# Gate/up product of a decoder block with its weights as the stationary operand and the tokens streamed

## The chip, the cores and the metric

The kernel runs on one core of a Trainium2 chip. The metric is the device time of one execution in microseconds (us), the median of three runs. Engines are named as the profile names them: PE is the matrix engine (PEld its weight loads), DVE, ACT and POOL work element by element, SP issues the loads of the weights.

A matmul on PE has two operands. The **stationary** one, a 128 x 128 tile, is loaded into the array first; the **moving** one is streamed through it, column by column. The result appears in PSUM, with one row for each column of the stationary tile and one column for each column of the moving operand.

## The reference

One decoder block for 256 tokens of width 1024: a convolution branch and an attention branch, merged and added to the input, and then the feed-forward part that the change is about.

```
h = h + merged @ w_out
n = h * rsqrt(mean(h * h) + EPS) * norm2_g
h = h + (silu(n @ w_gate) * (n @ w_up)) @ w_down      # w_gate, w_up: 1024 x 2816; w_down: 2816 x 1024
```

## The kernel before

**Three products for one.** All weights are float32. Each operand is split into a high part (rounded to the matmul type float32r) and a low part (the rest), and a product is summed from three matmuls: high by high, low by high, high by low. `mm3` issues them (L141, L142, L143).

**Slots.** The weights arrive in 146 pieces of 512 KB, 128 partitions by 1024 values, one for each slot. A list of slots, written out once, sets the order of all work. In each slot PE does 12 matmuls: two k-tiles, two token tiles, three matmuls each. Here a 128 x 128 tile of the tokens is stationary and 512 columns of a weight piece are streamed. Slots 0 to 79 are the products of the two branches and the out projection (80 x 12 = 960 such matmuls), slots 80 to 123 the gate/up product (528), and slots 124 to 145 the down product (246, and 36 with 256 columns, tile `end`, which finish the last block).

**Splitting.** ACT writes a piece's high part (`whi`, L123), DVE or POOL the low part (`wlo`, L124), six slots ahead of PE, into eight buffers each. In the built program these buffers lie 4,096 bytes apart in a partition.

**Between the products.** The out projection's result is added to the residual `xs`, transposed on PE (`htr`, L513) and split into `hh` and `hl` (L518, L519). The second norm's factor for each token, `rstd2`, comes from sums of squares on ACT (L525), one addition on DVE (L527) and two instructions on POOL (L178, L179). It is applied after the gate/up product, where a token is a row of the result, so the factor is one number for each partition.

**After a gate/up chunk.** Each chunk has 256 gate and 256 up columns. ACT takes silu of the gate half (L546), DVE multiplies (L548), giving `f` with tokens on the partitions. The down product wants `f` with its features on the partitions, so PE transposes it (`ftr`, L560, four in each of 11 chunks), and ACT and DVE split the result into `fh` and `fl` (L561, L562). The first two chunks are done in halves, so that h^T's second half may come later.

**Other work that the texts name.** `store` adds the down product to `xs` and writes the output (L571, L572). `ident` is the identity tile for transposes.

Of the kernel before, what the change touches and what calls it, by code (L numbers as in the profile page):

```python
# [26 lines left out]
G = 2  # L27
EPS = 1e-6
BIG = 1e30
# [11 lines left out]
SPL_BUFS = 8  # L41
AHEAD = 6
# [13 lines left out]
class Chunk:  # L56
    """CW output columns of one product, for all tokens: nk k-tiles in pieces of G."""

    def __init__(self, name, w, lhs, nk, done):
        self.name, self.w, self.lhs, self.nk, self.done = name, w, lhs, nk, done  # L60
        self.acc = None


@with_exitstack
def hybrid_block(ctx: ExitStack, tc: tile.TileContext, x, xT, par, w_in, w_co, w_ao, w_o, w_gu, w_dn, out):
# [20 lines left out]
    def add(*chunks):  # L86
        """One chunk, or two of which each half is done in turn."""
        n = chunks[0].nk // G
# [7 lines left out]

    def parts(i):
        return [slice(j, j + 1) for j in range(G)] if i < 3 else [slice(0, G)]

    def stream_dma(upto):  # L100
        while at["dma"] < min(upto, len(slots)):
            i = at["dma"]
            c, g = slots[i]
            raw[i] = wp.tile([P, G, CW], F32, tag="raw", bufs=RAW_BUFS, name=f"raw{i}")
# [8 lines left out]
    def stream_split(upto):  # L113
        while at["split"] < min(upto, len(slots)):
            i = at["split"]
            hi[i] = wp.tile([P, G, CW], F32R, tag="whi", bufs=SPL_BUFS, name=f"whi{i}")
            lo[i] = wp.tile([P, G, CW], F32R, tag="wlo", bufs=SPL_BUFS, name=f"wlo{i}")
            r = raw.pop(i)
            eng = nc.gpsimd if on_pool(i) else nc.vector
            for part in parts(i):  # L120
                if i == 0:
                    split_x(part.start)
                nc.scalar.copy(hi[i][:, part, :], r[:, part, :])  # L123
                eng.tensor_sub(lo[i][:, part, :], r[:, part, :], hi[i][:, part, :].bitcast(F32))  # L124
            at["split"] += 1
# [7 lines left out]
    def mm3(c, i, g, t, acc=None, cols=slice(0, CW), first=0, last=None):  # L133
        """Piece g of the chunk for token tile t; the sum runs from k-tile first to last."""
        xh, xl = c.lhs()
        acc = c.acc[t] if acc is None else acc
        last = c.nk - 1 if last is None else last
        tok = slice(t * P, (t + 1) * P)
        for j in range(G):
            k = g * G + j  # L140
            nc.tensor.matmul(acc, xh[:, k, tok], hi[i][:, j, cols], start=(k == first), stop=False)  # L141
            nc.tensor.matmul(acc, xl[:, k, tok], hi[i][:, j, cols], start=False, stop=False)  # L142
            nc.tensor.matmul(acc, xh[:, k, tok], lo[i][:, j, cols], start=False, stop=(k == last))  # L143

# [6 lines left out]
    warm = cst.tile([P, CW], BF16, name="warm")  # L151
# [7 lines left out]
    wps = bank("wps", CW)  # L159
    for _ in range(WARM):  # L160
        nc.tensor.matmul(wps, warm[:, :P], warm, start=True, stop=True)
# [14 lines left out]
    def rsqrt_mean(o, ss, n, width):  # L176
        """o = (ss / n + EPS) ** -0.5"""
# [27 lines left out]
    def refill(ch):  # L205
        """The channels of the next tile go on the partitions, after KC - 1 zeros."""
# [288 lines left out]
    s2 = sm.tile([P, T, 2], F32, bufs=1, name="s2")  # L495

    def out_done(b):
        cols = slice(b * CW, (b + 1) * CW)

        def done(slot, acc):  # L500
# [21 lines left out]
            def squares():  # L522
# [13 lines left out]
    ff = {}  # L536

    def ffn_done(c):
        def done(slot, acc):
            f = {}  # L540

            def gate():
                for t in range(T):
                    r = rstd2[:, t : t + 1]
                    sg = sm.tile([P, 256], F32, tag="e0", name=f"fs{c}{t}")
                    nc.scalar.activation(sg, acc[t][:, :256], AF.Silu, scale=r)  # L546
                    f[t] = sm.tile([P, 256], F32, tag="e1", name=f"f{c}{t}")
                    nc.vector.scalar_tensor_tensor(f[t], acc[t][:, 256:], r, sg, op0=ALU.mult, op1=ALU.mult)  # L548

            def turn():  # L550
                if not ff:
                    early.close()
                    late_pool = ctx.enter_context(tc.tile_pool(name="ff", bufs=1))
                    ff[0] = (late_pool.tile([P, KF, S], F32R, name="fh"), late_pool.tile([P, KF, S], F32R, name="fl"))
                fh, fl = ff[0]
                k2 = slice(2 * c, 2 * c + 2)
                tr = bank(f"ftr{c}", 2, S)
                for j in range(2):
                    for t in range(T):
# [4 lines left out]
            pre[slot + 1].append(gate)  # L564
            jobs[slot + 2].append(turn)
        return done
# [27 lines left out]
    ffn = [Chunk(f"gu{c}", w_gu[c], lambda: hT[0], KD, ffn_done(c)) for c in range(FF // 256)]  # L594
    add(*ffn[:2])
    for c in ffn[2:]:
        add(c)
# [26 lines left out]
    def square(q):  # L624
        """Squares of x, summed over the parts of its rows that share a partition."""
# [37 lines left out]
    for slot, (c, g) in enumerate(slots):  # L663
        for job in pre.pop(slot, ()):
            job()
        if g == 0:
            c.acc = [ps.tile([P, CW], F32, tag="mm", bufs=4, name=f"{c.name}_{t}") for t in range(T)]
        if slot < n - tail:
            mm3(c, slot, g, 0)
# [4 lines left out]
        if slot < n - tail:  # L674
            mm3(c, slot, g, 1, last=split_k - 1 if c is slots[-1][0] else None)
            if slot == n - tail - 1:
                nc.vector.tensor_add(xs[:, 1, D - CW :], xs[:, 1, D - CW :], c.acc[1])
# [17 lines left out]
        if g == c.nk // G - 1:  # L695
# [50 lines left out]
```

## Time and profile before

| | |
|---|---|
| median of 3 runs | 446.02 us (445.62 to 446.3) |
| span of the profiled execution | 443.5 us |
| time before and after that span, against the median | 2.5 us |
| PE busy | 437.6 us (99%), 2026 matmuls and as many loads |
| DVE, ACT, POOL busy | 309.6, 243.9, 87.5 us |

The profiled execution's own time is its span of 443.5 us from the first to the last instruction; the 2.5 us lie around it. A matmul's duration in the profile includes its way through the array, so what a stream of them costs is read from the distance between two starts. The chain of work that ended last says what the end of the program hangs on.

### The profile page before, as it was taken

The page shows a single profiled execution, that of the slowest core. Times are in us where ns is not written, and L with a number is a line of the kernel's source. Part 1 is how long each engine was busy: PE and PEld are TensorE (multiplying, and loading weights), DVE is VectorE, ACT ScalarE, POOL GpSimd, SP SyncE. Part 2 cuts the span into 40 slices and gives each one's busy share as a digit, 9 for nine tenths or more (in the row PEclk, how much of TensorE's full clock was granted, in tenths as well). Part 3 has the DMA queues.
Part 4 walks back from the last instruction along what each step waited for, and adds up shares of the span by engine and source line. Part 5 has one row for each costly group of instructions (what it writes and reads, how often), then busy time and mean ns, then how long its engine had stood idle before and what let it go on. Part 6 is the DMA issues. An engine that isn't in the chain of part 4 may idle for free.

```text
span 443.5 us, 5743 instructions
## 1 busy us (share of the span) xinstructions
PE 437.6 (99%) x2026; PEld 359.6 (81%) x2026; DVE 309.6 (70%) x523; ACT 243.9 (55%) x439; POOL 87.5 (20%) x73
## 2 busy tenths in 40 slices
PE   8999999999999999999999999999999999999997
PEld 4788888888888888888888888888888888888886
DVE  5989999898899799967586575555555555644501
ACT  6854466689998676639325374444444444633200
POOL 1614465745462443100000000000000000000000
PEclk9999999999999999999999999999999999999999
DMA  8986684355345444544837337655555555585001
GB/s 274 345 271 213 211 303 150 144 185 197 142 149 185 142 137 150 190 163 161 293 95 247 133 120 253 196 189 184 184 185 179 187 181 184 184 252 204 25 0 49
DMA packets 23340, 80.21 MB, mean 181 GB/s; under 512 B 2576, under 2 KB 3216, under 8 KB 23312
## 3 DMA queue, kind: packets, MB, share of 16 engines
q1 hardware_dynamic: 22896, 78.66, 52.9%
q10 hardware_dynamic: 416, 1.19, 0.8%
q8 instruction: 16, 0.26, 0.3%
q14 instruction: 12, 0.10, 0.1%
HBM read 78.79 MB, written 1.05 MB: 180 GB/s over the span
## 4 chain that ended last, share of the span: by engine, by line
PE 94%; POOL 2%; ACT 2%; DMA 1%; SPq 0%; issue 0%; DVE 0%
PE gu L141 9%; PE gu L143 9%; PE gu L142 9%; PE dn L141 4%; PE dn L143 4%; PE dn L142 4%; PE g L143 3%; PE g L142 3%; PE g L141 3%; PE conv L141 2%; PE conv L143 2%; PE conv L142 2%; PE k L143 2%; PE v L143 2%; PE q L143 2%; PE q L141 2%
## 5 line engine op out<-in xcount | busy, mean ns | idle before, releaser
L124 DVE TENSOR_TENSOR wlo<-raw,whi 128x1024 fp32r<-128x1024 f32 (+1 forms) x125 | 153.0, 1256 | 30.5 <-ACT whi L123 29.6
L123 ACT CAST whi<-raw 128x1024 fp32r<-128x1024 f32 (+1 forms) x149 | 148.9, 1035 | 34.9 <-PE dn L142 19.8
L221 DVE SCALAR_TENSOR_TENSOR cacc<-cv,prm,cacc 128x256 f32<-128x256 f32 x240 | 97.2, 475 | 0.2
L141 PE MATMUL gu<-whi,hh 128*128 128x512 f32 x176 | 69.6, 395 | 0.0
L124 POOL TENSOR_TENSOR wlo<-raw,whi 128x1024 fp32r<-128x1024 f32 x24 | 58.1, 2426 | 54.5 <-ACT whi L123 49.6
L143 PE MATMUL gu<-wlo,hh 128*128 128x512 f32 x176 | 68.7, 390 | 0.0
L142 PE MATMUL gu<-whi,hl 128*128 128x512 f32 x176 | 68.5, 389 | 0.0
L143 PEld LDWEIGHTS gu<-wlo,hh 128*128 128x128 f32 x176 | 33.0, 188 | 7.1
L142 PEld LDWEIGHTS gu<-whi,hl 128*128 128x128 f32 x176 | 33.1, 188 | 6.6
L141 PEld LDWEIGHTS gu<-whi,hh 128*128 128x128 f32 x176 | 33.1, 188 | 6.4
L141 PE MATMUL dn<-whi,fh 128*128 128x512 f32 x82 | 32.5, 396 | 0.0
L143 PE MATMUL dn<-wlo,fh 128*128 128x512 f32 x82 | 32.4, 396 | 0.0
L142 PE MATMUL dn<-whi,fl 128*128 128x512 f32 x82 | 32.4, 396 | 0.0
L546 ACT ACTIVATE fs<-gu,rstd 128x256 f32<-128x256 f32 x22 | 10.4, 475 | 39.1 <-PE gu L143 39.1
L548 DVE SCALAR_TENSOR_TENSOR f<-gu,rstd,fs 128x256 f32<-128x256 f32 x22 | 10.6, 484 | 29.1 <-ACT fs L546 29.1
L141 PE MATMUL conv<-whi,xgh 128*128 128x512 f32 x64 | 26.1, 409 | 0.9 <-ACT whi L123 0.8
L141 PE MATMUL g<-whi,xgh 128*128 128x512 f32 x64 | 26.6, 415 | 0.0
L142 PE MATMUL conv<-whi,xgl 128*128 128x512 f32 x64 | 25.4, 398 | 0.0
L143 PE MATMUL conv<-wlo,xgh 128*128 128x512 f32 x64 | 25.4, 397 | 0.0
L143 PE MATMUL g<-wlo,xgh 128*128 128x512 f32 x64 | 25.2, 394 | 0.0
L142 PE MATMUL g<-whi,xgl 128*128 128x512 f32 x64 | 25.0, 391 | 0.0
L561 ACT CAST fh<-ftr 128x512 fp32r<-128x512 f32 x11 | 6.5, 587 | 23.9 <-PE ftr L560 23.9
(159 smaller groups left out, 746.4 us busy)
## 6 DMA issues: line engine op xcount, KB each, us to landing
raw<-in_w_in SPq DMA_DIRECT2D x53, 512.0 KB, 4.2
raw<-in_w_gu SPq DMA_DIRECT2D x44, 512.0 KB, 4.3
raw<-in_w_dn SPq DMA_DIRECT2D x22, 512.0 KB, 4.1
raw<-in_w_ao SPq DMA_DIRECT2D x8, 512.0 KB, 3.3
raw<-in_w_co SPq DMA_DIRECT2D x8, 512.0 KB, 3.3
raw<-in_w_o SPq DMA_DIRECT2D x8, 512.0 KB, 5.1
raw<-in_w_in SPq DMA_DIRECT2D x6, 256.0 KB, 4.7
xs<-in_x ACTq DMA_DIRECT2D x1, 1024.0 KB, 4.7
```

Source lines behind the costliest of these rows:

```text
L123: nc.scalar.copy(hi[i][:, part, :], r[:, part, :])
L124: eng.tensor_sub(lo[i][:, part, :], r[:, part, :], hi[i][:, part, :].bitcast(F32))
L141: nc.tensor.matmul(acc, xh[:, k, tok], hi[i][:, j, cols], start=(k == first), stop=False)
L142: nc.tensor.matmul(acc, xl[:, k, tok], hi[i][:, j, cols], start=False, stop=False)
L143: nc.tensor.matmul(acc, xh[:, k, tok], lo[i][:, j, cols], start=False, stop=(k == last))
L221: nc.vector.scalar_tensor_tensor(cacc[j], src, w, cacc[j], op0=ALU.mult, op1=ALU.add)
L546: nc.scalar.activation(sg, acc[t][:, :256], AF.Silu, scale=r)
L548: nc.vector.scalar_tensor_tensor(f[t], acc[t][:, 256:], r, sg, op0=ALU.mult, op1=ALU.mult)
L561: nc.scalar.copy(fh[:, k2, :], tr)
```

## The change

The gate/up product is turned around. The 128 x 128 tiles of the weights become the stationary operand and h^T (`hh`, `hl`, 256 tokens) is streamed. A result tile then has 128 features on the partitions and 256 tokens along the row: the layout that the down product wants. There are 44 such column tiles, alternately gate and up, each the sum over 8 k-tiles and 3 matmuls: 1056 matmuls of 256 columns. A piece holds eight weight tiles, so a slot has 24 matmuls.

- The transposes `ftr` go. What follows a column tile is: gate times factor (`scaled`), silu, product with the up tile, high part, low part.
- The factor of the second norm is now one number for each column. `spread2` on POOL makes an all-ones tile and two diagonal tiles of `rstd2`, one matmul (`rb`, plain float32) turns them into a row for all partitions, and ACT copies it. It is applied to the gate alone; the up part's factor is applied at the end, in `store`.
- The first six column tiles take their first four k-tiles in slots 80 to 82 and the rest in slots 83 to 85; six PSUM banks are used in turn, two of them those of the convolution.
- The 16 buffers of split weights are 4,160 bytes apart, so that their addresses go through 0, 64, 128, ... modulo 512. In the built program `hh` moves from 0 to 256 modulo 512, and `fh` from 32 bytes past a multiple of 64 to a multiple of 64.
- A few small tiles change size (`warm`, `s2`).

```diff
+GU_BANKS = ("cv0", "cv1", "mm", "mm", "mm", "mm")
+GU_ORDER = halves_first(2 * KF, KD, len(GU_BANKS))
...
+    def spl(part, i):
+
+        u, n = shape_of(i)
+        t = wp.tile([P, G * CW + STEP], F32R, tag=f"w{part}{i % SPL_BUFS}", name=f"w{part}{i}")
+        return t[:, : G * CW].rearrange("p (u n) -> p u n", n=n)
...
-            hi[i] = wp.tile([P, G, CW], F32R, tag="whi", bufs=SPL_BUFS, name=f"whi{i}")
-            lo[i] = wp.tile([P, G, CW], F32R, tag="wlo", bufs=SPL_BUFS, name=f"wlo{i}")
+            hi[i], lo[i] = spl("hi", i), spl("lo", i)
...
+    def mm_cols(c, i, g, units, slot):
+        xh, xl = c.rhs()
+        for u in units:
+            n, k = c.order[g * U + u]
...
+            nc.tensor.matmul(acc, hi[i][:, u, :], xh[:, k, :], start=first, stop=False)
+            nc.tensor.matmul(acc, hi[i][:, u, :], xl[:, k, :], start=False, stop=False)
+            nc.tensor.matmul(acc, lo[i][:, u, :], xh[:, k, :], start=False, stop=last)
...
+                    spread2()
+                    jobs[slot + 4].append(row2)
...
-                    nc.scalar.activation(sg, acc[t][:, :256], AF.Silu, scale=r)
-                    nc.vector.scalar_tensor_tensor(f[t], acc[t][:, 256:], r, sg, op0=ALU.mult, op1=ALU.mult)
...
-                        nc.tensor.transpose(tr[:, j, t * P : (t + 1) * P], f[t][:, j * P : (j + 1) * P], ident)
-                nc.scalar.copy(fh[:, k2, :], tr)
-                nc.vector.tensor_sub(fl[:, k2, :], tr, fh[:, k2, :].bitcast(F32))
...
+    def spread2():
+
+        allone, diag = sm.tile([P, P], F32, tag="junk", name="allone"), free("diag")
+        nc.gpsimd.memset(allone, 1.0)
+        for t in range(T):
+            nc.gpsimd.tensor_scalar_mul(diag[:, t * P : (t + 1) * P], ident, rstd2[:, t : t + 1])
...
+    def row2():
+        rb = bank("rb", S)
+        nc.tensor.matmul(rb, second["ones"], second["diag"], start=True, stop=True)
+        second["row"] = free("row2", "kT")
+        nc.scalar.copy(second["row"], rb)
...
+            nc.vector.tensor_mul(st["g"], acc, second["row"])
...
+            nc.scalar.activation(st["s"], st["g"], AF.Silu)
...
+            nc.vector.tensor_mul(st["f"], acc, st["s"])
...
+            nc.scalar.copy(ff[0][0][:, j, :], st["f"])
...
+            nc.vector.tensor_sub(ff[0][1][:, j, :], st["f"], ff[0][0][:, j, :].bitcast(F32))
...
-        nc.vector.tensor_add(o, acc, xs[:, t, to])
+        nc.vector.scalar_tensor_tensor(o, acc, rstd2[:, t : t + 1], xs[:, t, to], op0=ALU.mult, op1=ALU.add)
```

On PE, inside the gate/up product, before (slot 83; `f` is the product of gate and up with tokens on the partitions):

```order
L141 MATMUL gu_0_2648<-whi_2658,hh 128x512
L142 MATMUL gu_0_2648<-whi_2658,hl 128x512
L143 MATMUL gu_0_2648<-wlo_2659,hh 128x512
L560 MATMUL ftr_2766<-ident,f_2724 128x128
L560 MATMUL ftr_2766<-ident,f_2728 128x128
L560 MATMUL ftr_2766<-ident,f_2724 128x128
L560 MATMUL ftr_2766<-ident,f_2728 128x128
L141 MATMUL gu_1_2649<-whi_2658,hh 128x512
```

and of the changed kernel, in the middle of slot 83, where the one extra matmul `rb` stands:

```order
L191 MATMUL gu_2585<-hh,whi_2531 128x256
L192 MATMUL gu_2585<-hl,whi_2531 128x256
L193 MATMUL gu_2585<-hh,wlo_2532 128x256
L606 MATMUL rb<-diag,allone 128x256
L191 MATMUL gu_2604<-hh,whi_2531 128x256
L192 MATMUL gu_2604<-hl,whi_2531 128x256
L193 MATMUL gu_2604<-hh,wlo_2532 128x256
```

The moving operand stands first behind the arrow: it was the weights, and is h^T now. The four transposes are gone, and `rb` stands 84 matmuls behind the product's first.

On POOL, the last work of the program, before and then now (`lr` belongs to the convolution's norm):

```order
L178 TENSOR_SCALAR lr<-mv 128x2
L179 TENSOR_TENSOR lr<-lr,mhalf 128x2
L178 TENSOR_SCALAR rstd_112<-rstd_112 128x2
L179 TENSOR_TENSOR rstd_112<-rstd_112,mhalf 128x2
L742 UNCONDITIONAL_BRANCH
```

```order
L231 TENSOR_TENSOR lr<-lr,mhalf 128x2
L230 TENSOR_SCALAR rstd_112<-rstd_112 128x2
L231 TENSOR_TENSOR rstd_112<-rstd_112,mhalf 128x2
L599 MEMSET allone 128x128
L601 TENSOR_SCALAR diag<-ident,rstd_112 128x128 x2
L831 UNCONDITIONAL_BRANCH
```

Three instructions now follow the factor on POOL, and `rb` on PE reads what they write.

On DVE, in the middle of the gate/up product, before and then now (`wlo` is the split of a later piece):

```order
L548 SCALAR_TENSOR_TENSOR f_2959<-gu_0_2876,rstd_112,fs_2957 128x256
L548 SCALAR_TENSOR_TENSOR f_2963<-gu_1_2877,rstd_112,fs_2961 128x256
L124 TENSOR_TENSOR wlo_2976<-raw_2856,whi_2975 128x1024
L124 TENSOR_TENSOR wlo_2994<-raw_2884,whi_2993 128x1024
L562 TENSOR_TENSOR fl<-ftr_2997,fh 128x512
L124 TENSOR_TENSOR wlo_3019<-raw_2902,whi_3018 128x1024
L124 TENSOR_TENSOR wlo_3037<-raw_2927,whi_3036 128x1024
```

```order
L617 TENSOR_TENSOR fg_2936<-gu_2903,row_2731 128x256
L157 TENSOR_TENSOR wlo_2954<-raw_2759,whi_2953 128x1024
L625 TENSOR_TENSOR f_2971<-gu_2938,fs_2969 128x256
L157 TENSOR_TENSOR wlo_2989<-raw_2795,whi_2988 128x1024
L635 TENSOR_TENSOR fl<-f_2971,fh 128x256
L617 TENSOR_TENSOR fg_3006<-gu_2973,row_2731 128x256
L157 TENSOR_TENSOR wlo_3024<-raw_2840,whi_3023 128x1024
L625 TENSOR_TENSOR f_3041<-gu_3008,fs_3039 128x256
```

Before, four splits came with three other instructions; now two come with three, and the three stand apart.

## Rows read from the trace of the kernel before

**Rows 1.** The page: busy time, granted clock by slice, chain that ended last.

```profile
PE 437.6 (99%) x2026; PEld 359.6 (81%) x2026; DVE 309.6 (70%) x523; ACT 243.9 (55%) x439; POOL 87.5 (20%) x73
...
PEclk9999999999999999999999999999999999999999
...
PE 94%; POOL 2%; ACT 2%; DMA 1%; SPq 0%; issue 0%; DVE 0%
```

**Rows 2.** Stretches: length, then PE, PEld, DVE, ACT, POOL busy, granted clock.

```profile
5.60:252.50 246.90, 246.25 (x1156) 203.90 (x1157) 210.35 (x412) 160.63 (x328) 84.75 (x58) 1.00 0.57 197
252.50:378.00 125.50, 125.50 (x579) 103.91 (x578) 73.30 (x85) 62.38 (x89) 0.89 (x2) 1.00 0.58 183
378.00:435.80 57.80, 57.80 (x251) 46.57 (x250) 23.62 (x22) 18.43 (x19) 0.00 (x0) 1.00 0.38 124
435.80:440.20 4.40, 4.40 (x37) 4.20 (x35) 1.12 (x2) 0.00 (x0) 0.00 (x0) 1.00 0.24 89
```

**Rows 3.** Timeline of PE in the gate/up product (start us, us).

```profile
299.81 0.39 PE L141 MATMUL gu<-whi,hh 128*128 128x512 f32 x1
...
302.30 0.39 PE L143 MATMUL gu<-wlo,hh 128*128 128x512 f32 x1
302.53 0.60 PE L560 MATMUL ftr<-ident,f 128*128 128x128 f32 x4
```

**Rows 4.** Timeline of PE in the down product.

```profile
400.80 0.40 PE L141 MATMUL dn<-whi,fh 128*128 128x512 f32 x1
...
402.20 0.40 PE L141 MATMUL dn<-whi,fh 128*128 128x512 f32 x1
```

**Rows 5.** Timeline of PE in the last 36 matmuls.

```profile
435.80 0.28 PE L141 MATMUL end<-whi,fh 128*128 128x256 f32 x1
...
439.94 0.28 PE L143 MATMUL end<-wlo,fh 128*128 128x256 f32 x1
```

**Rows 6.** The chain, pieces of the f transposes (start us, us, what).

```profile
291.32 0.44 PE ftr L560 x4
...
370.85 0.44 PE ftr L560 x4
```

**Rows 7.** Timeline of PE, transposes of the out projection.

```profile
256.65 1.04 PE L513 MATMUL htr<-ident,xs 128*128 128x128 f32 x8
257.44 0.48 PE L141 MATMUL gu<-whi,hh 128*128 128x512 f32 x1
```

**Rows 8.** Groups by line: weight loads of the eight warm-up matmuls.

```profile
L161 PEld LDWEIGHTS <-warm 128*128 128x128 bf16 x8 | 1.0, 141 | 2.8 <-issue 1.7 <-DVE warm L152 1.2
```

**Rows 9.** The chain, a plain float32 matmul of the scores.

```profile
91.50 0.43 PE sc L388 x2
```

**Rows 10.** Timeline of POOL, the second norm.

```profile
262.26 0.19 POOL L178 TENSOR_SCALAR rstd<-rstd 128x2 f32<-128x2 f32 x1 [67.14 <-DVE rstd L527]
262.54 0.69 POOL L179 TENSOR_TENSOR rstd<-rstd,mhalf 128x2 f32<-128x2 f32 x1
```

**Rows 11.** Groups by line on POOL: mean ns of one after the busy us.

```profile
L337 POOL TENSOR_SCALAR m<-m,rstd 128x4 f32<-128x4 f32 x8 | 2.8, 363 | 0.4
...
L633 POOL TENSOR_TENSOR sq<-sq 128x256 f32<-128x256 f32 x1 | 1.6, 1597 | 0.1
...
masks.py:197 POOL MEMSET ident<- 128x128 f32 x1 | 0.2, 204 | 0.3 <-POOLq L735 0.3
```

**Rows 12.** Timeline of DVE, the last part of h^T low.

```profile
260.79 0.48 DVE L519 SCALAR_TENSOR_TENSOR hl<-htr,prm,hh 128x256 fp32r<-128x256 f32 x1 [0.54 <-ACT hh L518]
```

**Rows 13.** Groups by line: the split, the product behind a chunk, a 256-column difference.

```profile
L124 DVE TENSOR_TENSOR wlo<-raw,whi 128x1024 fp32r<-128x1024 f32 x119 | 149.1, 1284 | 30.4 <-ACT whi L123 29.6 <-issue 0.7
...
L548 DVE SCALAR_TENSOR_TENSOR f<-gu,rstd,fs 128x256 f32<-128x256 f32 x22 | 10.6, 484 | 29.1 <-ACT fs L546 29.1
...
L424 DVE TENSOR_TENSOR aol<-pv,aoh 128x256 fp32r<-128x256 f32 x8 | 3.4, 422 | 0.5 <-ACT aoh L423 0.5
```

**Rows 14.** The chain, its last piece.

```profile
440.25 0.42 DVE o L571
```

More of the change, by code (lines that the diff above doesn't have):

```diff
@@ L28 @@
 EPS = 1e-6
+U = G * CW // P
 BIG = 1e30
@@ L41 @@
 SPL_BUFS = 8
+STEP = 16
 AHEAD = 6
@@ L61, in __init__, with halves_first @@
         self.acc = None
+class Cols:
+    def __init__(self, name, w, rhs, nk, order, done):
+        self.name, self.w, self.rhs, self.nk, self.order, self.done = name, w, rhs, nk, order, done
+        self.acc, self.seen = {}, defaultdict(int)
+def halves_first(cols, nk, first):
+    half = nk // 2
+    out = [(c, k) for ks in (range(half), range(half, nk)) for c in range(first) for k in ks]
+    return out + [(c, k) for c in range(first, cols) for k in range(nk)]
+GU_BANKS = ("cv0", "cv1", "mm", "mm", "mm", "mm")
+GU_ORDER = halves_first(2 * KF, KD, len(GU_BANKS))
 @with_exitstack
@@ L86, in add @@
     def add(*chunks):
+        if isinstance(chunks[0], Cols):
+            slots.extend((chunks[0], g) for g in range(len(chunks[0].order) // U))
+            return
         n = chunks[0].nk // G
@@ L95, in hybrid_block, with shape_of @@
     at = {"dma": 0, "split": 0}
+    def shape_of(i):
+        return (U, P) if isinstance(slots[i][0], Cols) else (G, CW)
     def parts(i):
-        return [slice(j, j + 1) for j in range(G)] if i < 3 else [slice(0, G)]
+        return [slice(j, j + 1) for j in range(G)] if i < 3 else [slice(None)]
     def stream_dma(upto):
@@ L103, in stream_dma @@
             c, g = slots[i]
-            raw[i] = wp.tile([P, G, CW], F32, tag="raw", bufs=RAW_BUFS, name=f"raw{i}")
+            raw[i] = wp.tile([P, *shape_of(i)], F32, tag="raw", bufs=RAW_BUFS, name=f"raw{i}")
             for part in parts(i):
@@ L148, in hybrid_block @@
     xs = cst.tile([P, T, D], F32, name="xs")
-    warm = cst.tile([P, CW], BF16, name="warm")
+    warm = cst.tile([P, P], BF16, name="warm")
     nc.vector.memset(warm, 0.0)
@@ L158, in hybrid_block @@
     load_table(AF.Sigmoid)
-    wps = bank("wps", CW)
+    wps = bank("wps", 4, P)
     for _ in range(WARM):
-        nc.tensor.matmul(wps, warm[:, :P], warm, start=True, stop=True)
+        nc.tensor.matmul(wps, warm, warm[:, None, :].to_broadcast([P, 4, P]), start=True, stop=True)
     ident = cst.tile([P, P], F32, name="ident")
@@ L492, in merge_done @@
         return done
-    s2 = sm.tile([P, T, 2], F32, bufs=1, name="s2")
+    s2 = sm.tile([P, 16], F32, bufs=1, name="s2")[:, : 2 * T].rearrange("p (t b) -> p t b", b=2)
     def out_done(b):
@@ new lines, in hybrid_block, with free @@
+    ff, gates, second = {}, {}, {}
+    def free(name, tag="qT"):
+        return sm.tile([P, S], F32, tag=tag, bufs=4, name=name)
+    def spread2():
[3 more added lines that the diff above has]
+            nc.gpsimd.tensor_scalar_mul(diag[:, t * P : (t + 1) * P], ident, rstd2[:, t : t + 1])
+        second["ones"], second["diag"] = allone, diag
+    def row2():
[3 more added lines that the diff above has]
+        nc.scalar.copy(second["row"], rb)
@@ L593, in hybrid_block @@
     add(*(Chunk(f"wo{b}", w_o[b], lambda: mT[0], KD, out_done(b)) for b in range(2)))
[L594 to L597, printed above, removed]
+    gu_slot = len(slots)
+    add(Cols("gu", w_gu, lambda: hT[0], KD, GU_ORDER, ffn_done))
     for b in range(2):
@@ L663, in hybrid_block @@
     for slot, (c, g) in enumerate(slots):
+        rows = isinstance(c, Chunk)
         for job in pre.pop(slot, ()):
             job()
-        if g == 0:
+        if not rows:
+            mm_cols(c, slot, g, range(U // 2), slot)
+        elif g == 0:
             c.acc = [ps.tile([P, CW], F32, tag="mm", bufs=4, name=f"{c.name}_{t}") for t in range(T)]
-        if slot < n - tail:
+        if rows and slot < n - tail:
             mm3(c, slot, g, 0)
@@ L673, in hybrid_block @@
             job()
-        if slot < n - tail:
+        if not rows:
+            mm_cols(c, slot, g, range(U // 2, U), slot)
+        elif slot < n - tail:
             mm3(c, slot, g, 1, last=split_k - 1 if c is slots[-1][0] else None)
             if slot == n - tail - 1:
-                nc.vector.tensor_add(xs[:, 1, D - CW :], xs[:, 1, D - CW :], c.acc[1])
+                end = xs[:, 1, D - CW :]
+                nc.vector.scalar_tensor_tensor(end, c.acc[1], rstd2[:, 1:2], end, op0=ALU.mult, op1=ALU.add)
             for job in post.pop(slot, ()):
@@ L694, in hybrid_block @@
         run_taps(slot, load["pe"] + LAG)
-        if g == c.nk // G - 1:
+        if rows and g == c.nk // G - 1:
             c.done(slot, c.acc)
@@ L708, in cols, with tiles @@
         return w.reshape(k // (G * P), G, P, n // CW, CW).transpose(3, 0, 2, 1, 4)
+    def tiles(w, order):
+        k, n = w.shape
+        w = w.reshape(k // P, P, n // P, P).transpose(2, 0, 1, 3)
+        return np.stack([w[c, j] for c, j in order]).reshape(-1, U, P, P).transpose(0, 2, 1, 3)
     def vec(v):
@@ L731 @@
         "w_o": cols(i["w_out"][0]),
-        "w_gu": cols(gu),
+        "w_gu": tiles(gu, GU_ORDER),
         "w_dn": cols(i["w_ffn_down"][0]),
```

58 lines of the change are left out of this document (35 added, 23 removed).

## The prediction

> **What bounds the kernel now.** I read the page first. PE is busy 99% of the span, 94% of the chain that ended last is PE, and the granted clock is at the upper of its two levels (2.4 GHz) in all slices [rows 1]. So the stretches have to be read, and in all three of the main ones PE's busy time is the whole stretch: the first 80 slots, the gate/up product and the down product [rows 2]. DVE is busy for 73 of 125.5 us in the gate/up product and ACT for 62. Nothing else waits long enough to matter: what counts is how long PE's stream of matmuls takes.
>
> The timelines give its pace, from start to start. In the gate/up product 12 matmuls of 512 columns lie between 299.81 and 302.53: 226.7 ns each [rows 3]. In the down product six lie between 400.80 and 402.20: 233.3 ns each [rows 4]. The last 36 have 256 columns; 35 steps between 435.80 and 439.94 are 118.3 ns each [rows 5]. At 2.4 GHz, 512 columns would stream in 213.3 ns and 256 in 106.7. So each matmul costs something beyond its columns: 13.4, 20.0 and 11.6 ns. The trace does not say what. The down product has the same shapes as the gate/up product; what differs in the program is the address of the stationary tile, 32 bytes past a multiple of 64 in `fh` and `fl`, at a multiple of 512 in `hh` and `hl`. I take it that the load of the next stationary tile disturbs the stream, and that addresses decide how much.
>
> **The change, part by part. All terms are on PE, so they add.**
>
> *The matmuls.* 528 of 512 columns at 226.7 ns are 119.7 us. They become 1056 of 256 columns, and 1056 loads: two of three use the same weight tile, but the eight warm-up matmuls with one tile show eight loads [rows 8], so a repeated tile is loaded again. No row has such a matmul in this place, so I bound it. Below: back-to-back transposes of 128 columns, each with a load; eight take 1.04 us and four 0.60, so one more takes 0.110 us [rows 3, 7]. Above: 106.7 plus the whole 13.4 ns that a 512-column matmul shows in this product, 120.1 ns. The nearest row is the 118.3 ns of the last 36 [rows 5], but those load from `fh`, where the 512-column pace is 233.3 and not 226.7. I take 118.3 x 226.7 / 233.3 = 115.0 ns: 121.4 us, **+1.7 us** (bounds -3.5 and +7.1).
>
> One rule of the notes speaks against this part. The Trainium skill ("TensorE: Matmul & The Clock Gate", section "LDWEIGHTS (loading the stationary operand)") lets a load take its columns divided by 1.2 GHz, an estimate of 107 ns for 128 columns: half of a 512-column matmul, but all of a 256-column one, so no slack is left behind which a load could hide. The 110 ns of the transposes agree with it. By it alone both forms would take 113 us (528 x 213.3 ns, 1056 x 107), and this term would be +0.4 instead of +1.7.
>
> *The transposes of f.* Seven chunks lie between the `ftr` pieces at 291.32 and 370.85 [rows 6]: 11.36 us each, of which 48 x 226.7 are 10.88. Four transposes cost 0.48 us, those in 11 chunks **-5.3 us**.
>
> *The row of factors.* `rb` is a plain float32 matmul of 256 columns; the chain shows 0.43 us for the two passes of such a matmul in the attention scores [rows 9], with the disturbance behind it **+0.5 us**. It also waits. The factor is ready on POOL at 262.54 + 0.69 = 263.23 [rows 10]. Then come the fill of a 128 x 128 tile, 0.20 us as for `ident`, and two products of 128 x 128 with a column of factors. For these I have a product with such a column over four values, 0.36 us, and a 256-column addition of 1.60 us [rows 11]; 128 columns with one tensor operand lie nearer the first. So `diag` is there at about 264.3 with 0.1 us of signalling (at the worst 266.7). PE comes to `rb` early. The transposes at 256.65 stand behind 18 matmuls, so the product began at 256.65 - 18 x 0.227 = 252.57; 84 matmuls of 0.115 us and 0.9 us for the eight transposes (0.79 to the next start, and a first matmul behind them of 0.48 instead of 0.39) [rows 3, 7] make 263.1. It waits 1.2 us (worst 3.6). Everything behind `rb` on PE waits with it, and all else is covered by the six slots that the split runs ahead: **+1.2 us**.
>
> *h^T's second half* is needed after 72 matmuls instead of four slots, at 252.57 + 0.9 + 8.3 = 261.8, its last k-tile 1 us later. `hl` ends at 260.79 + 0.48 = 261.27 [rows 12]. No wait; without the six tiles in halves it would be one of several us.
>
> *DVE and ACT.* DVE gains 44 multiplications of about 0.48 us and 22 differences of 0.42, loses 22 and 11 others of 0.48 and 0.69: some 12 us more in 125 [rows 13, 2]. It stays under 70% busy, so the splits of 1.28 us keep ahead. A column tile's bank is used again six slots later and is read within two or three. No cost.
>
> *The addresses.* `fh` now starts at a multiple of 64. If that is what the down product lacked, its 246 matmuls go from 233.3 to 226.7 and the last 36 by 3.3 ns: **-1.7 us** (bound 0). The split buffers also move for the 960 streamed matmuls of slots 0 to 79, through eight residues instead of one. The nearest rows are the two paces, 226.7 and 233.3, so between 0 and +6.3 us, and a gain can't be excluded, since even 226.7 is 13.4 above the columns. I take 0: neither row has the new residues.
>
> *The end.* The last `store` becomes the three-operand form, 0.48 us for 256 columns instead of 0.42 [rows 13, 14]: **+0.1 us**.
>
> **Sum:** 1.7 - 5.3 + 0.5 + 1.2 - 1.7 + 0.1 = -3.5 us. The profiled span is 443.5 us, 2.5 under the median of 446.02; with the same 2.5 the changed kernel takes **442.5 us**.
>
> **The rivals.** *Loads don't hold the stream (faster).* With weights at spread addresses a 256-column matmul costs the 110 ns of the transposes. That is -3.5 instead of +1.7 us; PE comes to `rb` 0.4 us earlier and waits as much longer: 437.7 us, and less if the first 80 slots gain too. For it: 110 ns is what a load and a short matmul were seen to take. Against: no 256-column row comes near it.
>
> *Addresses don't matter (slower).* Then the last 36 matmuls show the plain price of this shape, 118.3 ns: 124.9 us, +5.2. The down product keeps its 233.3, and PE waits 0.9 us. 5.2 - 5.3 + 0.5 + 0.9 + 0.1 = +1.4: **447.4 us**. For it: 118.3 is the only measured pace of the shape. Against: down and gate/up differ by 6.6 ns, and the program differs there in nothing else that I see. Without a gain in the down product the change loses from 117.0 ns a matmul on.
>
> The Trainium skill ("SBUF — State Buffer", section "Who interferes with whom") is on this rival's side: PE has separate read ports for the moving operand and for loads and never waits for another, so addresses would change nothing. The 226.7 against 233.3 ns of this trace do not fit it.
>
> *The spread addresses cost the streamed products (slower).* If the 960 matmuls go to the down product's 233.3 ns, +6.3: 448.8 us. It decides the sign from 3.6 ns a matmul on. For it: the one residue that differs in this trace is slower. Against: it differs by 32 bytes, the new ones by multiples of 64.
>
> *The row comes late.* POOL's two products at 1.6 us each: the wait is 3.6 instead of 1.2 us, 444.9 us.
>
> **How the numbers follow.** Chances: the forecast 0.38, loads that don't hold the stream 0.22, addresses that don't matter 0.14, streamed products slower 0.17, the late row 0.09. A measurement of this kernel tells about 0.2% (0.9 us) from no change. The forecast, the free loads and the late row are faster, together 0.69; but mixtures of them with the slower ones end within 0.9 us of 446.0, for which I take 0.07 from them and 0.03 from the slower: faster 0.62, same 0.10, slower 0.28. The range goes from 435.5, the free loads with 2 us more from the first 80 slots, to 449.0, just past the dearest rival; beyond it lie mixtures of the two slower ones. For the faster cases alone it is 437 to 445.
>
> **What would show it.** The gate/up stretch has no `ftr`, 1056 matmuls of 256 columns and one `rb`; starts 115 ns apart prove the first term, 110 or 118 a rival. PE should sit idle once, about 1 us, before `rb`, ended by POOL. The down product's starts show the address term (226.7 or 233.3), those of slots 0 to 79 whether the spread buffers cost anything. The prediction is wrong if the first 80 slots don't take 247 us again: that term is taken as 0 with no row behind it.

## The result, and the profile after

The changed kernel takes **452.1 us** (451.5 to 452.52, 4 runs) against 446.16 of the kernel before: a ratio of **1.0132**, 95% interval 1.0114 to 1.0149. It is 5.9 us slower where 3.5 us less were forecast. Its profiled execution has a span of 450.7 us.

The page of the changed kernel, with the rows that answer to [rows 1]:

```profile
PE 442.2 (98%) x2512; PEld 382.0 (85%) x2512; DVE 316.6 (70%) x556; ACT 245.7 (55%) x451; POOL 90.6 (20%) x76
...
PEclk8999999999999999999999998999999999999999
...
PE 92%; POOL 2%; ACT 2%; DMA 1%; DVE 1%; SPq 1%; POOLq 1%; issue 0%
```

PE is still what the program hangs on, but the clock is not up in all slices: the first and the 25th show 8 tenths (the first does so in the profiles of other kernels here, too). The stretches that answer to [rows 2] (length, then PE, PEld, DVE, ACT, POOL busy, granted clock):

```profile
5.20:255.90 250.70, 249.69 (x1157) 204.01 (x1158) 211.23 (x412) 160.76 (x328) 84.81 (x58) 0.99 0.57 194
255.90:385.60 129.70, 127.05 (x1067) 126.37 (x1066) 79.67 (x118) 65.53 (x103) 3.96 (x5) 0.99 0.54 176
385.60:443.00 57.40, 57.40 (x248) 46.31 (x248) 23.35 (x22) 16.92 (x17) 0.00 (x0) 1.00 0.39 129
443.00:447.40 4.40, 4.40 (x37) 4.19 (x35) 1.24 (x2) 0.00 (x0) 0.00 (x0) 1.00 0.24 89
```

Slots 0 to 79 take 250.7 us from the first matmul on instead of 246.9, the gate/up product 129.7 instead of 125.5, the down product 57.4 instead of 57.8. PEld is now busy for 126.4 of 129.7 us in the gate/up product: hardly a moment without a load. PE waits there for 2.7 us in all.

The pace of the gate/up matmuls alternates from slot to slot. In the timeline of PE, two stretches of 12 starts in neighbouring slots:

```profile
299.93 0.28 PE L192 MATMUL gu<-hl,whi 128*128 128x256 f32 x1
...
301.31 0.28 PE L192 MATMUL gu<-hl,whi 128*128 128x256 f32 x1
...
302.73 0.28 PE L192 MATMUL gu<-hl,whi 128*128 128x256 f32 x1
...
304.14 0.28 PE L192 MATMUL gu<-hl,whi 128*128 128x256 f32 x1
```

1.38 us for 12 are 115.0 ns each, 1.41 us are 117.5; over whole pairs of slots the mean is 116.8 ns. The streamed matmuls of the conv branch's output product, before and then now:

```profile
209.74 0.39 PE L141 MATMUL co<-whi,yh 128*128 128x512 f32 x1
...
211.55 0.39 PE L143 MATMUL co<-wlo,yh 128*128 128x512 f32 x1
```

```profile
211.61 0.39 PE L174 MATMUL co<-whi,yh 128*128 128x512 f32 x1
...
213.46 0.39 PE L176 MATMUL co<-wlo,yh 128*128 128x512 f32 x1
```

Eight took 1.81 us, 226 ns each; now they take 1.85 us, 231 ns each. The down product, for [rows 4]:

```profile
400.80 0.39 PE L176 MATMUL dn<-wlo,fh 128*128 128x512 f32 x1
...
402.19 0.39 PE L176 MATMUL dn<-wlo,fh 128*128 128x512 f32 x1
```

Six take 1.39 us, 232 ns; over the whole product it is 233.3 ns, as before, though now its pieces go at 232.2 and 234.5 ns in turn.

POOL and PE around `rb`, for [rows 10]:

```profile
266.22 0.69 POOL L231 TENSOR_TENSOR rstd<-rstd,mhalf 128x2 f32<-128x2 f32 x1
266.87 0.20 POOL L599 MEMSET allone<- 128x128 f32 x1
267.06 2.93 POOL L601 TENSOR_SCALAR diag<-ident,rstd 128x128 f32<-128x128 f32 x2
```

```profile
267.26 0.28 PE L193 MATMUL gu<-hh,wlo 128*128 128x256 f32 x1
270.04 0.70 PE L606 MATMUL rb<-diag,allone 128*128 128x256 f32 x2 [2.51 <-POOL diag L601]
270.39 0.47 PE L191 MATMUL gu<-hh,whi 128*128 128x256 f32 x1
...
271.37 0.41 PE L191 MATMUL gu<-hh,whi 128*128 128x256 f32 x1
271.58 0.41 PE L192 MATMUL gu<-hl,whi 128*128 128x256 f32 x1
```

The two products with a column of factors take 2.93 us on POOL, so `rb` starts 2.79 us after the matmul ahead of it. Its own passes and the matmul behind it are soon done, but then the matmuls start 0.21 us apart instead of 0.117. The stretches around this place show why (columns as above):

```profile
267.00:271.00 4.00, 1.49 (x11) 1.24 (x10) 2.00 (x2) 0.77 (x2) 2.99 (x3) 1.00 0.56 153
271.00:275.00 4.00, 4.00 (x23) 4.00 (x23) 1.98 (x3) 2.75 (x5) 0.00 (x0) 0.57 0.46 142
275.00:385.00 110.00, 110.00 (x944) 110.00 (x944) 68.53 (x101) 53.87 (x80) 0.00 (x0) 1.00 0.57 186
```

Between 271 and 275 us the granted clock is 0.57 of full speed: for most of this stretch PE ran at 1.2 instead of 2.4 GHz.

Last, the first matmuls of the gate/up product, which need h^T's first k-tiles at once:

```profile
257.21 0.39 PE L191 MATMUL gu<-hh,whi 128*128 128x256 f32 x1
257.73 0.39 PE L192 MATMUL gu<-hl,whi 128*128 128x256 f32 x1
```

0.52 us lie between these two starts. The first 24 matmuls lose some 0.8 us in such waits for `hh` and `hl`.

**The difference in parts.** From the starts of matmuls in the two profiles:

| part | forecast, us | measured, us |
|---|---|---|
| start of the program, up to slot 4 | 0 | +1.1 |
| rest of slots 0 to 79 | 0 | +2.2 |
| gate/up matmuls, 1056 at 116.8 ns | +1.7 | +3.7 |
| transposes of f (10 groups in this stretch, one behind it) | -5.3 | -5.3 |
| `rb` itself | +0.5 | +0.5 |
| wait of `rb` | +1.2 | +2.7 |
| low clock behind `rb` | - | +1.6 |
| waits for h^T's first k-tiles | - | +0.8 |
| down product's pace and the last 36 | -1.7 | 0.0 |
| end | +0.1 | 0.0 |
| sum of the parts | -3.5 | +7.3 |

The first line is not shown to be an effect of the change: over the profiles of this study slot 4 starts anywhere from 18.6 to 21.1 us, also in kernels that agree up to there. It may be one in part, though. The gate/up product begins at 255.7 to 257.0 us in the six profiles of kernels with the spread and at 252.6 to 253.3 in the six without it (the map of the residues left out), so up to there the spread may cost some 3 us instead of 2.2.

The spans differ by 7.3 us, the medians by 5.9. The profiled execution of the changed kernel is the slowest of its four, and not all have what it shows: in two of them the mean granted clock was 1.00 of full speed, so no stretch of theirs had the low clock. They took 451.5 and 451.74 us, the other two 452.46 and 452.52.

### The profile page after: what moved, and what is told of

It is laid out like the page before. It is cut to its first block, busy times and chain, and to the rows that moved or that the text cites. A ratio compares the mean times of both kernels' runs of the same rounds, so it can differ in the third digit from the quotient of the medians.

```text
span 450.7 us, 6858 instructions
## 1 busy us (share of the span) xinstructions
PE 442.2 (98%) x2512; PEld 382.0 (85%) x2512; DVE 316.6 (70%) x556; ACT 245.7 (55%) x451; POOL 90.6 (20%) x76
## 4 chain that ended last, share of the span: by engine, by line
PE 92%; POOL 2%; ACT 2%; DMA 1%; DVE 1%; SPq 1%; POOLq 1%; issue 0%
PE gu L192 9%; PE gu L193 9%; PE gu L191 9%; PE dn L175 4%; PE dn L176 4%; PE dn L174 4%; PE g L176 3%; PE g L174 3%; PE g L175 3%; PE conv L174 2%; PE conv L175 2%; PE conv L176 2%; PE co L174 2%; PE ao L174 2%; PE q L174 2%; PE v L174 2%
## 5 line engine op out<-in xcount | busy, mean ns | idle before, releaser
L157 DVE TENSOR_TENSOR wlo<-raw,whi 128x1024 fp32r<-128x1024 f32 (+1 forms) x125 | 155.2, 1258 | 27.0 <-ACT whi L156 25.9
L192 PE MATMUL gu<-hl,whi 128*128 128x256 f32 x352 | 99.4, 282 | 0.1
L193 PE MATMUL gu<-hh,wlo 128*128 128x256 f32 x352 | 99.1, 281 | 0.0
L191 PE MATMUL gu<-hh,whi 128*128 128x256 f32 x352 | 98.8, 281 | 0.0
L193 PEld LDWEIGHTS gu<-hh,wlo 128*128 128x128 f32 x352 | 67.3, 191 | 0.0
L192 PEld LDWEIGHTS gu<-hl,whi 128*128 128x128 f32 x352 | 66.8, 190 | 0.4 <-DVE hl L571 0.3
L191 PEld LDWEIGHTS gu<-hh,whi 128*128 128x128 f32 x352 | 66.8, 190 | 0.3 <-ACT hh L570 0.2
L625 DVE TENSOR_TENSOR f<-gu,fs 128x256 f32<-128x256 f32 x22 | 9.3, 424 | 24.1 <-PE gu L193 24.1
L621 ACT ACTIVATE fs<-fg 128x256 f32<-128x256 f32 x22 | 9.3, 421 | 30.5 <-DVE fg L617 30.5
L617 DVE TENSOR_TENSOR fg<-gu,row 128x256 f32<-128x256 f32 x22 | 9.3, 425 | 21.7 <-PE gu L193 19.5
```

The lines of the kernel that those rows point to most:

```text
L191: nc.tensor.matmul(acc, hi[i][:, u, :], xh[:, k, :], start=first, stop=False)
L192: nc.tensor.matmul(acc, hi[i][:, u, :], xl[:, k, :], start=False, stop=False)
L193: nc.tensor.matmul(acc, lo[i][:, u, :], xh[:, k, :], start=False, stop=last)
L617: nc.vector.tensor_mul(st["g"], acc, second["row"])
L621: nc.scalar.activation(st["s"], st["g"], AF.Silu)
L625: nc.vector.tensor_mul(st["f"], acc, st["s"])
```

## The experiments

**Theory**: a matmul pays for the load that runs beside it, and how much depends on the residue between the address of the tile being loaded and that of the tile being streamed. The spread buffers give the streamed products worse residues. The rest is the wait for `diag` and what it does to the clock. **Rival**: addresses don't matter; the losses are the price of 256 columns and something at the start.

### Only the spread

```diff
-            hi[i] = wp.tile([P, G, CW], F32R, tag="whi", bufs=SPL_BUFS, name=f"whi{i}")
-            lo[i] = wp.tile([P, G, CW], F32R, tag="wlo", bufs=SPL_BUFS, name=f"wlo{i}")
+            hi[i], lo[i] = spl("hi", i), spl("lo", i)
```

> The kernel before with only the split buffers 4,160 bytes apart (and the smaller warm-up tile that makes room for it); the gate/up product is the old one. Theory, spread addresses cost the streamed matmuls some 2.5 ns each: slots 0 to 79 take 2.3 us longer (starts about 229.5 ns apart instead of 227), gate/up 1.3 us longer, the down product stays near 233 ns; in all 449.5 to 450. Rival, addresses don't matter and the loss in slots 0 to 79 is something of the start: 446.1, and slots 4 to 79 take what they took.

450.64 us, ratio 1.0099 (1.0083 to 1.0116). Its stretches:

```profile
5.40:255.80 250.40, 249.46 (x1157) 203.94 (x1158) 211.18 (x413) 160.79 (x329) 84.76 (x58) 0.99 0.57 195
255.80:383.10 127.30, 127.30 (x578) 103.86 (x577) 73.20 (x85) 62.26 (x89) 0.89 (x2) 1.00 0.56 180
383.10:440.70 57.60, 57.60 (x252) 46.52 (x251) 23.59 (x22) 18.38 (x19) 0.00 (x0) 1.00 0.37 124
```

The gate/up product takes 127.3 instead of 125.5 us, and slots 4 to 79 take 2.1 us more (part of the rest is the start). Nothing but addresses of tiles has changed here, bar the form of the warm-up tile. So addresses do matter: the spread alone costs the old kernel 4.6 us, 0.6 above what was expected. What it is worth in the changed kernel is the next question.

### The change without the spread

```diff
-STEP = 16
+STEP = 0
```

> The changed kernel with the split buffers 4,096 bytes apart: every weight tile and every tile of h^T then starts at the same residue modulo 512. Theory: slots 0 to 79 lose their 2.3 us; the gate/up matmuls all go at the pace of the pieces that have this residue now, 118.1 ns instead of a mean of 116.8, +1.4 us; the down product's stationary tiles stand 64 bytes past the weights' residue, pace unknown; in all about 451. Rival, addresses don't matter: 452.1 and gate/up pieces alternate no more or less than now.

452.9 us, ratio 1.0152 (1.0134 to 1.017). Slots 4 to 79 are back at 234.0 us, as before. But the gate/up product is slower:

```profile
299.87 0.28 PE L191 MATMUL gu<-hh,whi 128*128 128x256 f32 x1
...
301.31 0.28 PE L191 MATMUL gu<-hh,whi 128*128 128x256 f32 x1
```

Twelve take 1.44 us: 120.0 ns each, all slots alike, where 118.1 was expected. So in the changed kernel the spread pays for itself: 3.2 ns on each of 1056 gate/up matmuls are 3.4 us, against the 2 to 3 us that it costs ahead of them. At the same residue a 512-column matmul of the kernel before took 226.7. Each is 13.3 ns above its columns at 2.4 GHz (106.7 and 213.3): here what comes on top is the same whatever the width. The alternating pace is gone, as the theory has it. In this kernel `fh` starts 64 bytes past the weights' residue, and the last 36 matmuls say something else:

```profile
441.87 0.28 PE L174 MATMUL end<-whi,fh 128*128 128x256 f32 x1
...
445.84 0.28 PE L176 MATMUL end<-wlo,fh 128*128 128x256 f32 x1
```

35 steps in 3.97 us are 113.4 ns, though the 512-column matmuls just ahead, at the same residue, stay at 233.3. `rb` waits here too:

```profile
264.65 0.28 PE L193 MATMUL gu<-hh,wlo 128*128 128x256 f32 x1
267.31 0.70 PE L606 MATMUL rb<-diag,allone 128*128 128x256 f32 x2 [2.38 <-POOL diag L601]
...
267.96 0.28 PE L192 MATMUL gu<-hl,whi 128*128 128x256 f32 x1
268.08 0.28 PE L193 MATMUL gu<-hh,wlo 128*128 128x256 f32 x1
```

It comes 2.66 us after the matmul ahead of it, and the matmuls behind it are 0.12 us apart: no low clock in this execution. It is the shortest of the five, 451.23 us at a mean granted clock of 1.00; the other four took 452.88 to 453.02 at 0.992 to 0.996. Their clock was low somewhere, the record doesn't say where.

### The diagonal tiles on DVE

```diff
-        nc.gpsimd.memset(allone, 1.0)
+        nc.vector.memset(allone, 1.0)
...
-            nc.gpsimd.tensor_scalar_mul(diag[:, t * P : (t + 1) * P], ident, rstd2[:, t : t + 1])
+            nc.vector.tensor_scalar_mul(diag[:, t * P : (t + 1) * P], ident, rstd2[:, t : t + 1])
```

> The changed kernel with the all-ones tile and the two diagonal tiles made on DVE instead of POOL. Theory, the wait of 2.7 us before rb also brought the clock down for the matmuls behind it (about 24 at 213 instead of 117 ns, 2.2 us): both go, 447.2. Rival, the low clock there comes from something else and stays: 449.4. If the wait is covered by other slack: 452.1.

448.53 us, ratio 1.0055 (1.0039 to 1.007). The gate/up product goes from 129.8 to 125.8 us in the profile: `rb` no longer waits, and no low clock follows. The medians differ by 3.6 us, between the rival (2.7) and the theory (4.9), and nearer to the rival. That fits the executions of the changed kernel: two of four had no low clock, so their median holds about half of its 1.6 us, and 2.7 + 0.8 = 3.5 us is what the step should give (an estimate).

### `rb` half a slot later

```diff
-                    jobs[slot + 4].append(row2)
+                    pre[slot + 5].append(row2)
```

> The changed kernel with rb 12 matmuls later, at the start of slot 84. The wait shrinks from 2.7 to about 1.3 us. Theory, the length of the wait brings the clock down: with 1.3 us the clock stays up and 1.4 + 2.2 us are saved, 448.5. Rival, any wait of PE there lowers the clock: only 1.4 us are saved, 450.7.

449.75 us, ratio 1.0081 (1.0065 to 1.0096), between the two.

```profile
268.51 0.28 PE L193 MATMUL gu<-hh,wlo 128*128 128x256 f32 x1
269.92 0.70 PE L606 MATMUL rb<-diag,allone 128*128 128x256 f32 x2 [1.13 <-POOL diag L601]
...
270.57 0.28 PE L192 MATMUL gu<-hl,whi 128*128 128x256 f32 x1
270.69 0.28 PE L193 MATMUL gu<-hh,wlo 128*128 128x256 f32 x1
```

The wait is 1.3 us, and the clock stays up behind it: 0.12 us between starts. The gate/up product takes 2.9 us less than in the changed kernel, of which the shorter wait is 1.4.

### A map of the residues

```diff
+    def residue(i):
+        if i < 8:
+            return 0
+        if i < gu_slot:
+            return (i // 4) % 16
+        if i < gu_slot + 44:
+            return ((i - gu_slot) // 2) % 16
+        return (i - gu_slot - 44) % 16
...
+        at_ = 8 * residue(i)
+        return t[:, at_ : at_ + G * CW].rearrange("p (u n) -> p u n", n=n)
```

> The kernel of e3_after_diag_dve with each piece's split buffers moved by a multiple of 32 bytes, so that all 16 residues modulo 512 between the loaded tile and the streamed one come in turn: by 4 slots in slots 8 to 79, by 2 in the gate/up product, by 1 in the down product (7 buffers instead of 8 make room). Theory, the residue between the tile being loaded and the tile being streamed sets what a load costs: the gate/up pace is near 120 ns at 0 (seen with no spread), near 113 at +64 (the last 36 matmuls there) and at +128, and repeats after 256; the streamed products are at 226.7 at 0 and at 233 for +32 and +64, other residues unknown. Rival, not the residue but the changing of residues from buffer to buffer costs: then all constant stretches of two and four slots run alike, near 117 and 227 ns.

450.35 us in one run. Mean distance of starts in ns, by the residue of the loaded tile less that of the streamed one, modulo 512 (steps above 260 and 200 ns left out, and for the down product those at a piece's edge):

```
residue, bytes      0    32    64    96   128   160   192   224   256   288   320   352   384   416   448   480
down, 512 col.  226.7 232.2 233.0 233.7 233.4 234.6 228.9 233.3 226.7 232.2 232.9 233.8 233.4 234.6 231.1 232.0
gate/up, 256    120.8 118.5 115.8 118.7 118.7 119.8 117.8 117.8 119.8 118.5 117.8 117.4 118.7 119.8 117.8 117.8
```

512-column matmuls are best at 0 and 256 and pay 2 to 8 ns more elsewhere. 256-column ones are at their worst there, near 120 ns, and as bad at 160 and 416, where the 512-column ones are at their worst too. So at 0 the two shapes are opposite, but not everywhere. At 128, where some 113 ns were expected for 256 columns, 118.7 were measured. The map nearly repeats after 256 bytes for 512 columns and, but for 64 and 96, for 256. The rival of the expectation, that change itself costs, falls: constant stretches differ.

The lowest entry, 115.8 at 64, is the mean of two visits to that residue, one right behind `rb` and one late in the product (slots 85 and 117):

```profile
272.82 0.28 PE L201 MATMUL gu<-hh,whi 128*128 128x256 f32 x1
...
275.54 0.28 PE L201 MATMUL gu<-hh,whi 128*128 128x256 f32 x1
```

```profile
363.78 0.28 PE L201 MATMUL gu<-hh,whi 128*128 128x256 f32 x1
...
366.61 0.28 PE L201 MATMUL gu<-hh,whi 128*128 128x256 f32 x1
```

In each, 24 steps: 2.72 us are 113.3 ns each, 2.83 us are 117.9. At 96, too, the two visits differ: 120.0 ns in slots 86 and 87, 117.4 in slots 118 and 119. So 64 is best in one visit and no better than other residues in the other, and the residue alone does not set the pace of this shape.

### Residues chosen for each product

```diff
-STEP = 16
+STEP = 0
...
+        at_ = 48 if name == "h" else 0
+        return tuple(
+            t8.tile([P, KD * S + 64], F32R, tag="t8" + p, name=name + p)[:, at_ : at_ + KD * S]
+            .rearrange("p (k s) -> p k s", s=S)
+            for p in "hl"
+        )
...
+                late_pool.tile([P, PAD], F32, name="pad")
```

It keeps the diagonal tiles on DVE.

> The kernel of e3_after_diag_dve without the spread, with h^T 192 bytes on (weight tiles then start 64 bytes past it, modulo 256) and the down product's fh and fl moved to the weights' residue. Theory, residues alone set the paces: slots 0 to 79 as before (some 2.1 us less than e3), gate/up 115.8 ns (1.1 us less), down 226.7 ns (1.6 us less): 443.7. Rival, the map's stretches don't carry over to a whole product: 446 to 448.

**440.98 us, ratio 0.9891 (0.9878 to 0.9905)**: faster than the kernel before, and 2.7 us better than expected. The stretches:

```profile
5.40:252.90 247.50, 246.07 (x1156) 203.92 (x1157) 210.35 (x411) 160.64 (x328) 84.77 (x58) 0.99 0.57 196
252.90:375.40 122.50, 122.36 (x1068) 121.65 (x1067) 79.97 (x121) 65.82 (x104) 0.89 (x2) 1.00 0.56 187
375.40:431.20 55.80, 55.80 (x248) 46.23 (x248) 23.35 (x22) 16.97 (x17) 0.00 (x0) 1.00 0.40 133
```

The gate/up product takes 122.5 us, the down product 55.8 (226.7 ns a matmul). The gate/up pace is 113.3 ns behind `rb`, not the map's 115.8. The timeline ahead of `rb` and behind it:

```profile
261.07 0.28 PE L194 MATMUL gu<-hh,whi 128*128 128x256 f32 x1
...
264.25 0.28 PE L194 MATMUL gu<-hh,whi 128*128 128x256 f32 x1
...
265.98 0.28 PE L194 MATMUL gu<-hh,whi 128*128 128x256 f32 x1
...
267.68 0.28 PE L194 MATMUL gu<-hh,whi 128*128 128x256 f32 x1
```

Ahead, 27 matmuls take 3.18 us, 117.8 ns each; behind, 15 take 1.70, 113.3 each, and it stays there to the product's end. The addresses are the same on both sides, and the two paces are those of the map's two visits to 64. So a residue does not fix one pace: the stream has settled into another rhythm behind the disturbance. Not every disturbance does that: the eight transposes of h^T's second half, 36 matmuls into the product, left it at 117.8.

### The kernel before with `fh` moved

```diff
+                    late_pool.tile([P, PAD], F32, name="pad")
```

> The kernel before with one pad of 480 bytes ahead of fh and fl, so that they start at the weights' residue. Theory, the 32 bytes are all that made the down product slower than the gate/up product: 226.7 instead of 233.4 ns for 246 matmuls, 1.6 us less, 444.4, and the last 36 at 120 instead of 118.3 ns, 0.1 more. Rival, the down product is slow for another reason: 446.1.

444.29 us, ratio 0.9964 (0.9952 to 0.9977): a pad of 480 bytes saves 1.5 us of the kernel before.

```profile
399.99 0.39 PE L142 MATMUL dn<-whi,fh 128*128 128x512 f32 x1
...
401.80 0.39 PE L144 MATMUL dn<-wlo,fh 128*128 128x512 f32 x1
```

Eight matmuls of the down product take 1.81 us, 226 ns each, where [rows 4] show 233.3. So its slowness was the residue, as the prediction took it to be, but the residue against the weights (32 before, 0 with the pad), not that against a multiple of 64.

### h^T's first k-tiles later

```diff
-    out = [(c, k) for ks in (range(half), range(half, nk)) for c in range(first) for k in ks]
+    out = [(c, k) for k in range(half) for c in range(4)]
+    out += [(c, k) for c in range(4, first) for k in range(half)]
+    out += [(c, k) for c in range(first) for k in range(half, nk)]
```

> The kernel of e6_residues_chosen with the first halves of four column tiles done k-tile by k-tile, so that h^T's k-tiles 1 to 3 are needed later. Theory, the short waits for hh and hl in the first matmuls of the gate/up product (0.7 us beyond their pace) go: 0.7 us less than e6_residues_chosen. Rival, the waits only move: the same.

440.42 us, ratio 0.9873 (0.9858 to 0.9888). The gate/up product is 0.4 us shorter in the profile: the first waits are gone, but PE comes earlier to `rb` and waits 0.4 us there, for DVE now. The interval overlaps that of the kernel without this edit, so by the medians alone it is not shown. It is the best version measured.

### The wait again, and a longer one

The first has no edit, the second makes the two diagonal tiles twice:

```diff
-        for t in range(T):
+        for t in (0, 1, 0, 1):
```

> The changed kernel itself once more, for a second look at the wait before rb. If the wait of 2.7 us always brings the clock down behind it, some 24 matmuls behind rb start 213 ns apart again; the kernel without the spread had a wait of 2.6 us with the clock up, so the other outcome, all at 117 ns and a gate/up stretch of about 128 us, is as likely.

451.84 us (two runs, 452.43 and 451.24). `rb` waits 2.8 us as before. In the profiled one the granted clock falls at 269.7 us, 0.4 us before `rb` starts: the two passes of `rb` are 0.59 us apart instead of 0.32, and 8 steps behind it take 0.21 us each, where the first profile had 16. The other execution has a mean clock of 1.00 and so no low clock at all.

> The changed kernel with the two diagonal tiles made twice on POOL, so that rb waits 2.9 us longer, 5.7 in all. Theory, a wait this long surely brings the clock down: the gate/up stretch takes 2.9 us more than 129.8, and 213 ns starts stand behind rb as before, at least as many. Rival, the low clock has nothing to do with the wait: none behind rb.

454.16 us (two runs). POOL took 4.1 us for the four products, not 5.9, so the start of `rb` is 3.9 us behind the matmul ahead of it, and 15 steps of 0.21 us follow. In the profiles a wait of 2.66 us went once without the low clock; waits of 2.79 (twice) and 3.9 us had it. But with the wait of 2.79 us three of the six executions of the changed kernel have a mean clock of 1.00, so a wait of this length makes the low clock possible, not sure.

### A disturbance on purpose

```diff
+    pre[gu_slot + 1].append(lambda: nc.tensor.matmul(bank("kick", S), ident, xs[:, 0, :S], start=True, stop=True))
```

> The kernel of e6_residues_chosen with one more plain float32 matmul, which nothing reads, after the first slot of the gate/up product. There the matmuls ahead of rb start 117.8 ns apart and those behind it 113.3, at the same residues. Theory, a disturbance of the stream lets it settle at the lower pace: 113.3 ns from slot 81 on, 57 matmuls ahead of rb. Rival, something else changes at rb: 117.8 ns until rb as before.

441.49 us (two runs).

```profile
257.58 0.28 PE L194 MATMUL gu<-hh,whi 128*128 128x256 f32 x1
...
258.49 0.28 PE L196 MATMUL gu<-hh,wlo 128*128 128x256 f32 x1
```

Eight steps in 0.91 us: 113.8 ns behind the extra matmul, and 113.3 up to `rb`, where the kernel without it went at 117.8. The theory held: the stream has two steady paces at the same addresses, and what came before decides which it takes. Why this matmul moves it and eight transposes don't is open. The time is no shorter for it: 57 matmuls at 4.5 ns less are 0.26 us, and the extra matmul costs more.

## Why the prediction was wrong

**What bounds the kernel** was read rightly: PE, and the pace of its stream. The step to "the load of the next stationary tile disturbs the stream, and addresses decide how much" was right as far as the addresses go, and no more than argued there; the pad ahead of `fh` shows it. That it is the load that disturbs, no run shows apart from the addresses.

**The gate/up pace** failed in the step "I take 118.3 x 226.7 / 233.3 = 115.0 ns". It carried the ratio between two residues from 512 columns over to 256. The runs show the opposite order: at residue 0 the 512-column matmul is at its best (226.7) and the 256-column one at its worst (120.0). The upper bound of 120.1, "106.7 plus the whole 13.4 ns", is what the change without the spread measured (120.0). With the spread it became 116.8 ns, +3.7 instead of +1.7 us. The Trainium skill ("TensorE: Matmul & The Clock Gate", section "LDWEIGHTS (loading the stationary operand)") has a load of 128 columns take 107 ns, an estimate from its formula. No gate/up pace of these runs came under it, but none came to it either; 113.3 was the best, and whether the load's length sets that pace is not shown.

**The addresses** failed twice. "I take 0" for the streamed products of slots 0 to 79: the spread cost 2.2 us there, within the stated bounds of 0 and 6.3. The rival "the spread addresses cost the streamed products" was right, at a third of its price (half of it, if the later start belongs to the spread). And the -1.7 us in the down product did not come: `fh` at a multiple of 64 was not the point, the residue against the streamed weights is, and under the spread no piece went at 226.7. The rule of the Trainium skill ("SBUF — State Buffer", section "Who interferes with whom") that PE's two read ports are independent and that PE never waits for another does not fit these runs, if it is taken to mean that addresses change nothing: 480 bytes of padding changed 246 matmuls by 6.5 ns each. The experiments don't tell what the two streams share.

**The wait of `rb`** was seen, with its cause and its place, but sized at 1.2 us instead of 2.7: "128 columns with one tensor operand lie nearer the first" of the two rows. The products took 1.47 us each, near the second. That is the rival "the row comes late", at three fifths of its price (1.5 of 2.4 us more). What no rival held is the clock: the longer wait was followed by a stretch at 1.2 GHz, 1.6 us in the profile, though in at most three of six executions. With the tiles on DVE the profile shows neither.

**h^T.** "No wait" looked at the second half alone. The new order needs four k-tiles of the first half within 12 short matmuls, and lost 0.8 us.

**The top of the range**, 449.0, was "just past the dearest rival", with one rival at a time. Here the streamed products, the gate/up pace and the late row each came true in part, and the clock and h^T on top of them.

**Right** were the transposes (-5.3), `rb` itself, the repeated loads (1056 loads), DVE and ACT out of the way, and the end.

**The turned product itself can be worth having.** With a residue chosen for each product and `diag` on DVE it takes 122.4 us against 125.4, and 441.0 us in all against 444.3 of the old form with its down product mended. The loss came mostly from addresses and one late tile. But that lead hangs on the lower pace, which the residue alone did not give: at 117.8 ns to its end the product would take 972 x 4.5 ns = 4.4 us more, an estimate, and the lead would be gone. That the pace fell was luck, though all three profiles of this form end at the lower one.

## What to carry to other kernels

When matmuls stream without a gap, compare start-to-start times of equal shapes: a difference of a few ns that no engine explains points at the addresses of loaded and streamed tiles, and one run that steps through residues gives a first map for each shape. Try the best residue on a whole product before believing it, because the same addresses can have two paces. A price measured for one width must not be scaled to another. Before a matmul is made to wait for a chain on another engine, take that chain's price from an instruction of the same form or bound it by the worst, and count what the clock may do behind the wait.

## What the runs showed that was not expected

- At one set of addresses the stream of 256-column matmuls has two steady paces, 117.8 and 113.3 ns. A single plain float32 matmul in between moved it to the lower one for the rest of the product; eight transposes did not.
- 512-column matmuls are at their best and 256-column ones at their worst at residue 0 (226.7 and 120.0 ns); at 64 they take 233.3, and 113.3 or 117.8.
- Two float32 products of 128 x 128 values with a column of factors took 2.93 us on POOL, four in a row 4.1 us: no fixed price each.
- The low clock does not stand at a fixed place behind a wait. Behind 2.79 us, four steps went at 112 to 118 ns before 16 at 213; in another execution the clock fell before the wait ended, and 8 steps behind it went at 213; in three of six it did not fall.
